# A hybrid attention and DeltaNet layer on one core: gate columns loaded first, the inverse doubled for both chunks at once, scores in two passes

## The chip, the cores and the metric

The kernel runs on one core of a Trainium2 chip. The core has a matrix engine (TensorE, PE in the profile) and three elementwise engines (VectorE or DVE, ScalarE or ACT, GpSimd or POOL). SyncE (SP) issues DMAs. Each engine takes its instructions in the order in which they were written. Times are device microseconds (us) of one execution; the runs of the kernel before took 190.68, 192.27 and 193.10 us, median 192.27.

## What is computed

One decoder layer on x of 256 tokens by 1,024 columns. x is normalised and multiplied with one matrix `w_in` of 4,104 columns, which holds ten inputs: q, k, v, z of eight attention heads (`aq`, `ak`, `av`, `az`, 512 columns each), q, k, v, z of four DeltaNet heads (`dq`, `dk`, `dv`, `dz`, 512 each), and eight gate columns.

```python
h = rms_norm(x, norm_pre_w)
proj = h @ w_in
moba_out = moba_attention(q, k, v) * silu(a_z)        # causal softmax with ALiBi, 8 heads of 64
qkv = silu(causal_depthwise_conv(concat([d_q, d_k, d_v]), conv_w))
beta = sigmoid(d_b)
g = -exp(a_log) * softplus(d_a + dt_bias)
o = gated_delta_rule(q, k, v, g, beta)                # 4 heads of 128, chunked
gdn_out = rms_norm(o, gdn_norm_w) * silu(d_z)
mixed = concat([moba_out, gdn_out]) @ w_out
return x + rms_norm(mixed, norm_post_w)
```

In the delta rule each chunk needs the inverse of a unit lower triangular matrix, and the decays between its tokens:

```python
decay = exp(where(causal, gc[:, None] - gc[None, :], -inf))    # gc: cumulated g
a = where(strict, (k * beta) @ k.T * decay, 0)
t_inv = triangular_solve(a + eye, eye)
```

## The kernel before

The kernel uses two chunks of 128 tokens (t = 0, 1) and writes all work into a plan (`Plan.record`, line 149). `Plan.order` simulates the engines with its own costs, latencies and clock model, ranks what is ready, and `Plan.emit` writes every instruction in the order found. So the order of the code below is not the order of the engines' queues; each is an outcome of the planner, and nearly all instructions have the line of the helper, L364, in the profile. They are told apart by the names of their tiles.

Precision is kept by splitting fp32 operands into two fp32r parts, `hi` (an ACT copy) and `lo` (a DVE subtraction), and by three matmuls per product: hi by hi, hi by lo, lo by hi. A product of plain fp32 operands is one instruction in the code and two records in the profile.

Head (lines 421 to 568). SP loads x in four halves, `wrow` (the norm weight, as one row), then the last 264 columns of `w_in` in four pieces (`dz_raw`): 256 columns of z and the eight gate columns. 18 matmuls of zeros (`ps_warm`) are marked `late`, to be used when PE has nothing else. GpSimd builds all constants: identity, triangles, the masks `blk`, `blks`, `lvl`, the attention bias `bias0`, `qscale`, and later `sel`. The norm weight is spread over the partitions by two matmuls (`ps_w`), DVE scales x by it and by the row's rsqrt (lines 555 to 557), PE transposes the sixteen 128x128 blocks of x (`hT`), and ACT and DVE evict them as `hhi` and `hlo`, 512 columns at a time.

Projections. `dz_piece(1)` (line 628) multiplies the 264 gate and z columns; `dz_piece(0)`, called at line 898, loads and multiplies the other 256 z columns. `proj_group` (line 590) does 512 columns in 96 matmuls; its weights come as two loads of 1 MB, `raw`, from four buffers.

Gates and decay (lines 654 to 702). A chain of small instructions gives `bet` and `gneg`. For each chunk the exponents `ps_d` come from one bf16 matmul for the upper triangle and, per head, a DVE product `gs` of `strl` with the head's gate and an fp32 matmul of `gs` with `triu`.

Inverse (lines 768 to 872). `msk` (GpSimd) and `cmp` pick the 16x16 diagonal blocks, `ps_gb` spreads their rows, and DVE inverts all blocks of both chunks in 15 steps of a product (`wprod`) and a sum (`wc`). `wT` holds the inverse, `xX` its transpose. Then blocks are doubled from 16 to 32, 64 and 128: for each chunk by itself, PE makes `ps_y`, ACT copies it to `yz`, PE makes `ps_w` and DVE subtracts it from `wT`. `xX` is kept up in the same way with products `ps_x` of its own. GpSimd makes the masked `ns` for the first level and clears `yz`.

Recurrence and attention. Lines 901 to 953 run the two chunks of the delta rule (`ps_p`, `ps_S`, `ps_o`). For attention (lines 956 to 1022) `ps_s` holds a head's scores: for the first 128 queries one fp32 matmul, for the other 128 three fp32r matmuls (`qh` by `kh`, `qh` by `kl`, `ql` by `kh`). Both use 64 of the 128 array rows, as a head has 64 channels. Softmax is DVE and ACT work; `ps_pt` are transposes of the weights.

End. `w_out` comes in four loads of 1 MB; `ps_out` adds up the DeltaNet half first, then the attention half. The norm, the residual x and the stores follow, all stores from SP's queue.

Of the kernel before, what the change touches and what calls it, by code (L numbers as in the profile page):

```python
# [8 lines left out]
F32 = mybir.dt.float32  # L9
# [102 lines left out]
class Op:  # L112
    __slots__ = ("n", "eng", "call", "args", "kw", "cost", "table", "preds", "succs", "bufs", "start", "end", "pin", "late", "boost", "work", "load", "pass_")
# [10 lines left out]
class Plan:  # L124
# [9 lines left out]
    def __init__(self):  # L134
        self.ops, self.slots, self.counts, self.boost = [], {}, {}, 0
# [13 lines left out]
    def record(self, eng, real, name, args, kw):  # L149
# [6 lines left out]
        op.boost = self.boost  # L156
# [8 lines left out]
        op.work = op.load = op.pass_ = 0.0  # L165
        if eng == "pe":
# [5 lines left out]
            k = views[1].box[0][1] - views[1].box[0][0]  # L172
            op.work = k / P
        op.preds, op.succs, op.bufs = {}, [], []
        if after:
            op.preds[self.ops[-1]] = True
# [19 lines left out]
    def cost(eng, name, views, kw):  # L196
# [11 lines left out]
        if eng == "dve":  # L208
            if name == "tensor_reduce":
                n = max(v.size() for v in views)  # L210
            ap = 60 * (name == "tensor_scalar" and len(views) > 2 or name == "scalar_tensor_tensor" and n > 64)
# [10 lines left out]
        row = (v.box[-1][1] - v.box[-1][0]) * 4  # L222
        return max(400, (v.box[0][1] - v.box[0][0]) * v.size() * 4 / (370 if row >= 2048 else 220))

    def run(self, rank, banks, reverse=False):
# [26 lines left out]
        table, load, last = None, 1.0, 0.0  # L252
        window, done, cold, share, self.low = 0, {}, True, 1.0, 1.0
        for _ in range(len(ops)):
            best = None
            for e, todo in ready.items():
                cand = []
                for op in todo:
                    t = max(at[op], free[e])
                    if e == "pe":  # L260
                        t = max(t, last + op.load)
# [8 lines left out]
                if not cand:  # L270
# [3 lines left out]
                    (c for c in cand if c[0] <= t0 + (SLACK if e == "pe" else 1)),  # L274
                    key=lambda c: (-1e9 if c[1].pin else 1e9 if c[1].late else rank[c[1]] - c[1].boost 
# [13 lines left out]
            c = op.cost  # L289
            if op.eng == "pe" and not reverse:  # L290
# [79 lines left out]
SLACK = 20  # L370
TABLE = 2000
# [4 lines left out]
GATES = 1  # L376
WARM = 18
# [3 lines left out]
def tile_hybrid(  # L381
# [32 lines left out]
    w_cols = w_in[0].rearrange("(kt p) n -> p kt n", p=P)  # L414
# [3 lines left out]
    wrow = sl("s4", [1, D], "wrow")  # L418
    sv = const([49, P], "sv")
# [3 lines left out]
    dz_raw = plan.tile(sb, [P, KT, PIECE + 2 * HG], F32, "raw_dz1", tag="raw", bufs=RAW_BUFS)  # L423
    HD = D // 2
    for t in range(NT):
# [10 lines left out]

    KH = KT // 2
    GROUP = 2 * PIECE
# [11 lines left out]
    wz = const([P, 256], "wz", BF16)  # L450
    V.memset(wz, 0.0, pin=True)
    pz = bank([P, 512], "ps_warm")
    for i in range(WARM):
        PE.matmul(pz[:, :256], wz[:, :P], wz[:, :256], start=True, stop=True, late=True)


    ident = const([P, P], "ident")
# [10 lines left out]
    blk = const([P, NB, BASE], "blk")  # L468
    G.memset(blk, 1.0)
    G.affine_select(out=blk, in_=blk, pattern=[[-BASE, NB], [0, BASE]], compare_op=OP.is_ge,  # L470
                    fill=0.0, base=0, channel_multiplier=1)
    G.affine_select(out=blk, in_=blk, pattern=[[BASE, NB], [0, BASE]], compare_op=OP.is_ge,
                    fill=0.0, base=BASE - 1, channel_multiplier=-1)

    blks = const([P, NB, BASE], "blks")
    G.affine_select(out=blks, in_=blk, pattern=[[BASE, NB], [1, BASE]], compare_op=OP.is_gt,
                    fill=0.0, base=0, channel_multiplier=-1)

# [649 lines left out]
```

## Time and profile before

| what | value |
|---|---|
| median of three runs | 192.27 us |
| profiled execution | 193.22 us |
| its span, first to last instruction | 191.5 us |
| mean granted PE clock | 0.917 |
| matmul records | 1,337 |
| moved by DMA | 24.92 MB, mean 130 GB/s |

The span leaves out about 1.7 us around the program. Busy times of PE are pipelined spans, so the pace of a run of matmuls is better read from the chain of work: its length over its number of records. The granted clock is the share of full speed that PE was given; at 0.5 a matmul takes twice as long. A row of stretches gives busy time by engine, with the number of instructions in brackets.

### The profile page before, as it was taken

The page shows a single profiled execution, that of the slowest core. Times are in us where ns is not written, and L with a number is a line of the kernel's source. Part 1 is how long each engine was busy: PE and PEld are TensorE (multiplying, and loading weights), DVE is VectorE, ACT ScalarE, POOL GpSimd, SP SyncE. Part 2 cuts the span into 40 slices and gives each one's busy share as a digit, 9 for nine tenths or more (in the row PEclk, how much of TensorE's full clock was granted, in tenths as well). Part 3 has the DMA queues.
Part 4 walks back from the last instruction along what each step waited for, and adds up shares of the span by engine and source line. Part 5 has one row for each costly group of instructions (what it writes and reads, how often), then busy time and mean ns, then how long its engine had stood idle before and what let it go on. Part 6 is the DMA issues. An engine that isn't in the chain of part 4 may idle for free.

```text
span 191.5 us, 3512 instructions
## 1 busy us (share of the span) xinstructions
PE 179.7 (94%) x1337; PEld 163.5 (85%) x1337; DVE 132.5 (69%) x327; ACT 102.1 (53%) x215; POOL 26.4 (14%) x60
## 2 busy tenths in 40 slices
PE   6879999999979999999999999999999999999970
PEld 3359999999969999878977999999888999888860
DVE  3679479995999999984122377627849997725463
ACT  4446499679555666332110364426768989632230
POOL 8546000000580030000000031500000000000100
PEclk9955999999999999997555699999999999999999
DMA  5878998479821634492710000651290000630023
GB/s 168 240 258 242 270 341 295 109 172 259 241 62 23 196 73 151 87 246 109 163 56 3 0 0 3 219 173 46 104 338 0 5 0 0 203 129 0 0 110 110
DMA packets 13448, 24.92 MB, mean 130 GB/s; under 512 B 582, under 2 KB 2935, under 8 KB 13432
## 3 DMA queue, kind: packets, MB, share of 16 engines
q1 hardware_dynamic: 13432, 24.71, 43.5%
q8 instruction: 10, 0.16, 0.3%
q14 instruction: 6, 0.05, 0.1%
HBM read 23.65 MB, written 1.05 MB: 129 GB/s over the span
## 4 chain that ended last, share of the span: by engine, by line
PE 69%; DVE 14%; issue 5%; DMA 4%; ACT 3%; SPq 3%; POOLq 0%; POOL 0%; DVEq 0%
PE ps_out L364 9%; PE ps_ak L364 6%; PE ps_az L364 6%; PE ps_dk L364 6%; PE ps_aq L364 6%; PE ps_av L364 6%; PE ps_dz L364 4%; DMA sv<-in_gdn_norm_w_dram 4%; PE ps_w L364 4%; PE ps_dq L364 3%; PE ps_y L364 3%; PE ps_s L364 3%; SPq L364 3%; DVE y_dv L364 2%; PE ps_gb L364 2%
## 5 line engine op out<-in xcount | busy, mean ns | idle before, releaser
L364 DVE TENSOR_TENSOR o_lo<-raw_o,o_hi 128x1024 fp32r<-128x1024 f32 x8 | 9.8, 1224 | 5.6 <-ACT o_hi L364 5.6
L364 ACT ACTIVATE o_hi<-raw_o 128x1024 fp32r<-128x1024 f32 x8 | 8.5, 1058 | 5.1 <-PE ps_out L364 4.8
L364 ACT ACTIVATE yz<-ps_y 32x128 f32<-32x128 f32 (+2 forms) x8 | 2.6, 324 | 16.0 <-PE ps_w L364 8.9
L364 ACT ACT_TABLE_LOAD x8 | 10.3, 1283 | 0.9 <-PEq L1115 0.8
L364 DVE TENSOR_TENSOR wT<-wT,ps_w 32x128 f32<-32x128 f32 (+2 forms) x8 | 2.8, 349 | 11.1 <-PE ps_w L364 10.0
L364 PE MATMUL ps_dz<-dz_lo,hhi 128*128 128x264 f32 (+1 forms) x32 | 10.4, 326 | 0.0
L364 PE MATMUL ps_dz<-dz_hi,hhi 128*128 128x264 f32 (+1 forms) x32 | 10.3, 321 | 0.0
L364 PE MATMUL ps_dz<-dz_hi,hlo 128*128 128x264 f32 (+1 forms) x32 | 10.0, 312 | 0.0
L364 PEld LDWEIGHTS ps_w<-wT,yz 32*32 32x32 f32 (+2 forms) x64 | 7.9, 207 | 2.4 <-issue 1.3
L364 POOL TENSOR_TENSOR pr<-pr,pow-1_89 128x1 f32<-128x1 f32 x2 | 1.1, 558 | 63.3 <-DVE pr L364 63.3
L364 PE MATMUL ps_az<-hlo,az_hi 128*128 128x256 f32 x32 | 9.5, 297 | 0.0
L364 PE MATMUL ps_az<-hhi,az_hi 128*128 128x256 f32 x32 | 9.5, 295 | 0.0
L364 PE MATMUL ps_az<-hhi,az_lo 128*128 128x256 f32 x32 | 9.3, 290 | 0.0
L364 PE MATMUL ps_ak<-hhi,ak_lo 128*128 128x256 f32 x32 | 9.2, 287 | 0.0
L364 PE MATMUL ps_dv<-hlo,dv_hi 128*128 128x256 f32 x32 | 9.2, 286 | 0.0
L364 PE MATMUL ps_dq<-hhi,dq_hi 128*128 128x256 f32 x32 | 9.2, 286 | 0.0
L364 PE MATMUL ps_aq<-hhi,aq_hi 128*128 128x256 f32 x32 | 9.1, 286 | 0.0
L364 PE MATMUL ps_dq<-hhi,dq_lo 128*128 128x256 f32 x32 | 9.1, 284 | 0.0
L364 PE MATMUL ps_ak<-hhi,ak_hi 128*128 128x256 f32 x32 | 9.1, 284 | 0.0
L364 PE MATMUL ps_ak<-hlo,ak_hi 128*128 128x256 f32 x32 | 9.1, 283 | 0.0
L364 PE MATMUL ps_aq<-hlo,aq_hi 128*128 128x256 f32 x32 | 9.0, 282 | 0.0
L364 PE MATMUL ps_aq<-hhi,aq_lo 128*128 128x256 f32 x32 | 9.0, 282 | 0.0
(264 smaller groups left out, 669.4 us busy)
## 6 DMA issues: line engine op xcount, KB each, us to landing
raw_o<-in_w_out_dram SPq DMA_DIRECT2D x4, 1024.0 KB, 5.0
raw_dk<-in_w_in_dram SPq DMA_DIRECT2D x2, 1024.0 KB, 10.2
raw_dq<-in_w_in_dram SPq DMA_DIRECT2D x2, 1024.0 KB, 11.0
raw_dv<-in_w_in_dram SPq DMA_DIRECT2D x2, 1024.0 KB, 10.2
raw_av<-in_w_in_dram SPq DMA_DIRECT2D x2, 1024.0 KB, 8.3
raw_aq<-in_w_in_dram SPq DMA_DIRECT2D x2, 1024.0 KB, 5.9
raw_ak<-in_w_in_dram SPq DMA_DIRECT2D x2, 1024.0 KB, 6.6
raw_az<-in_w_in_dram SPq DMA_DIRECT2D x2, 1024.0 KB
```

What stands on the lines that cost most here:

```text
L364: op.call(*args, **kw)
```

## The change

1. *Head.* All 520 columns of `dz` and gates come first, in eight loads with rows of 2,080 bytes. `w_in`'s rows are dealt to partitions as `(p kt)` instead of `(kt p)`, so x is transposed with a step of eight columns and the norm weight is a value per partition (`wcol`), applied in the eviction of each 128x128 block. The matmuls `ps_w` and the scaling of x by them go; x is scaled by the row's rsqrt alone, half on ACT and half on DVE. 48 late matmuls instead of 18.
2. *GpSimd's constants.* The masks, the bias, `qscale` and the clearing of `yz` wait for a small copy (`held`) of the gate columns. `sel` is now an ACT copy of the identity.
3. *Decay.* The gates are split into two fp32r parts; per chunk and part one DVE product of 512 columns and one fp32r matmul.
4. *Masks.* `msk` and `ns` are made by DVE instead of GpSimd.
5. *Doubling.* Both chunks in each instruction (eight heads). The `ps_x` products go; `xX` is made by DVE transposes of `wT`.
6. *Scores.* A head's q hi and q lo stand on the two halves of the partitions, k hi on both, k lo on one with zeros on the other: each query block takes two fp32r matmuls over 128 rows.
7. *End.* The second store of each chunk is issued from ACT's queue.
8. *Planner.* Margins on every hand-over, a price for a change of the array rows used, other DMA costs, and leads by stage (`LEAD`) in place of one boost for the gates.

```diff
+LEAD = {"out0": 3258, "dk": 12754, "inv": -3594, "dbl": -402, "out1": -1204, "att0": -192, "mixd": 1425, "az": -11589, "dz": -5411, "gates": 158, "vt": -3052}
-WARM = 18
+SWITCH = 90
+BATCH = 752
+MARGIN = [411, 175, 0]
+WARM = 48
...
-    w_cols = w_in[0].rearrange("(kt p) n -> p kt n", p=P)
+    w_cols = w_in[0].rearrange("(p kt) n -> p kt n", p=P)
...
-    for t in range(NT):
-        for c0 in (0, HD):
-            SP.dma_start(xs[t][:, c0 : c0 + HD], x[0, t * P : (t + 1) * P, c0 : c0 + HD], pin=True)
-        if t == 0:
-            SP.dma_start(wrow, norm_pre_w, pin=True)
-    for k in range(0, KT, 2):
-        SP.dma_start(dz_raw[:, k : k + 2, :], w_cols[:, k : k + 2, 3840:], pin=True)
+    for t in range(NT):
+        SP.dma_start(xs[t], x[0, t * P : (t + 1) * P, :], pin=True)
+    SP.dma_start(wcol, norm_pre_w[0].rearrange("(p kt) -> p kt", kt=KT), pin=True)
+    for k in range(KT):
+        SP.dma_start(dz_raw[k // KH][:, k % KH, :], w_cols[:, k, 3584:], pin=True)
...
-        for i in range(2):
-            xh = xs[t][:, i * HD : (i + 1) * HD]
-            V.scalar_tensor_tensor(xh, xh, r, wps[i], op0=OP.mult, op1=OP.mult)
+        A.activation(xs[t][:, :HD], xs[t][:, :HD], AF.Copy, scale=r)
+        V.tensor_scalar(xs[t][:, HD:], xs[t][:, HD:], r, None, op0=OP.mult)
...
-            A.activation(hhi[at], ps, AF.Copy)
-            V.tensor_tensor(hlo[at], ps, hhi[at], OP.subtract)
+                w = wcol[:, kt : kt + 1]
+                A.activation(hhi[at], ps[:, k, :], AF.Copy, scale=w)
+                V.scalar_tensor_tensor(hlo[at], ps[:, k, :], w, hhi[at], op0=OP.mult, op1=OP.subtract)
...
+            for t in range(NT):
+                token_mms(z1[t], zh[:, k, PIECE:], zl[:, k, PIECE:], kt, t, st, sp)
+            for t in range(NT):
+                token_mms(z0[:, t, :], zh[:, k, :PIECE], zl[:, k, :PIECE], kt, t, st and t == 0, sp and t == NT - 1)
...
+    G.tensor_copy(const([P, 2 * HG], "held"), ba[:, 0, :])
+    now = plan.ops[-1]
...
-        PE.matmul(pd, ident16, far16[:, None, :].to_broadcast(HB), start=True, stop=False)
-        for h in range(HG):
-            V.tensor_scalar(gs[:, h, :], strl, gneg[:, t, h : h + 1], None, op0=OP.mult)
-            PE.matmul(pd[:, h, :], gs[:, h, :], triu, start=False, stop=h == HG - 1)
+        for i in range(2):
+            gs = gsa[i][:, of_chunk[t], :]
+            V.tensor_tensor(gs, triu[:, None, :].to_broadcast(HB), gpart[i][:, t, :, None].to_broadcast(HB), OP.mult)
+            PE.matmul(pd, strl, gs, start=i == 0, stop=False)
+        PE.matmul(pd, ident16, far16[:, None, :].to_broadcast(HB), start=False, stop=True)
...
+    py = bank([P, NH, 64], "ps_y16")
+    for h in range(NH):
+        PE.matmul(py[:, h, :], nsa[:, h, :], head_cols(xXa, 0, h), start=True, stop=True)
+    A.activation(half_cols(yz16, 0), py.rearrange("p h (n s) -> p h n s", n=n), AF.Copy)
+    pw = bank([P, NH, 64], "ps_w16")
+    for h in range(NH):
+        PE.matmul(pw[:, h, :], yz16[:, h, :], head_cols(wTa, 1, h), start=True, stop=True)
+    hc = half_cols(wTa, 1)
+    V.tensor_tensor(hc, hc, pw.rearrange("p h (n s) -> p h n s", n=n), OP.subtract)
+    for t in range(NT):
+        transpose32(t)
...
+        V.tensor_tensor(wTa[r1, :, r2], wTa[r1, :, r2], pw[r1], OP.subtract)
+        if b == 0:
+            V.transpose(xXa[r2, :, r1], wTa[r1, :, r2])
...
+            for e in range(2):
+                b, b2 = own[e], own[1 - e]
+                ps, qs_ = qps[half][b, c, :], qscale[b, m : m + 1]
+                A.activation(q[b, e, :], ps, AF.Copy, scale=qs_)
+                V.scalar_tensor_tensor(q[b2, e, :], ps, qs_, q[b, e, :], op0=OP.mult, op1=OP.subtract)
+                ps = kps[half][b, c, :]
+                A.activation(kh[b, e, :], ps, AF.Copy)
+                A.activation(kh[b2, e, :], ps, AF.Copy)
+                V.tensor_tensor(kl[b, e, :], ps, kh[b, e, :], OP.subtract)
...
-                PE.matmul(ps_s[:, :P], qa[b, m, :], ka[b, m, :], start=True, stop=True)
-                PE.matmul(ps_s[:, P:], qh[b, m, :], kh[b, m, :], start=True, stop=False)
-                PE.matmul(ps_s[:, P:], qh[b, m, :], kl[b, m, :], start=False, stop=False)
-                PE.matmul(ps_s[:, P:], ql[b, m, :], kh[b, m, :], start=False, stop=True)
+                for o, ts, ks in ((ps_s[:, :P], slice(0, P), slice(0, P)), (ps_s[:, P:], slice(P, T), slice(0, T))):
+                    PE.matmul(o, q[:, ts], kh[:, ks], start=True, stop=False)
+                    PE.matmul(o, q[:, ts], kl[:, ks], start=False, stop=True)
...
-            SP.dma_start(out[0, t * P : (t + 1) * P, cs], u[:, cs])
+            (AQ if i == 1 else SP).dma_start(out[0, t * P : (t + 1) * P, cs], u[:, cs])
```

More of the change, by code (lines that the diff above doesn't have):

```diff
@@ L112 @@
 class Op:
-    __slots__ = ("n", "eng", "call", "args", "kw", "cost", "table", "preds", "succs", "bufs", "start", "end", "pin", "late", "boost", "work", "load", "pass_")
+    __slots__ = ("n", "eng", "call", "args", "kw", "cost", "table", "preds", "succs", "bufs", "start", "end", "pin", "late", "boost", "work", "load", "pass_", "stage", "rows")
 class Queue:
@@ L466, in tile_hybrid @@
                     fill=0.0, base=0, channel_multiplier=-1)
[L468 to L477, printed above, removed]
-    strl = const([P, P], "strl")
+    strl = const([P, P], "strl", F32R)
     G.affine_select(out=strl, in_=ones, pattern=[[-1, P]], compare_op=OP.is_gt,
@@ L539, in tile_hybrid @@
     cols = columns(sv, 49, "cols")
-    wps = [bank([P, HD], f"ps_w{i}") for i in range(2)]
-    for i in range(2):
-        PE.matmul(wps[i], ones[0:1, :], wrow[:, i * HD : (i + 1) * HD], start=True, stop=True)
     ssq = const([P, NT, 2], "ssq")
@@ L605, in proj_group, with token_mms, token_piece @@
         return pss
-    def token_piece(raw, n, name, fine):
+    def token_mms(o, hi, lo, kt, t, first, last):
+        ts = slice(t * P, (t + 1) * P)
+        PE.matmul(o, hhi[:, kt, ts], hi, start=first, stop=False)
+        PE.matmul(o, hhi[:, kt, ts], lo, start=False, stop=False)
+        PE.matmul(o, hlo[:, kt, ts], hi, start=False, stop=last)
+    def token_piece(raw, n, name, kn, fine):
         banks = [bank([P, n], f"ps_{name}_{t}") for t in range(NT)]
-        kn = 2 if n > 2 * PIECE - 1 else KH
         for kg in range(0, KT, kn):
@@ new lines, in tile_hybrid @@
+    nl = P // (2 * BASE)
+    lvl = const([P, nl, 2, BASE], "lvl")
+    G.memset(lvl[:, :, 0, :], 0.0, after=now)
+    G.memset(lvl[:, :, 1, :], 1.0, after=now)
+    G.affine_select(out=lvl[:, :, 1, :], in_=lvl[:, :, 1, :], pattern=[[-2 * BASE, nl], [0, BASE]],
+                    compare_op=OP.is_ge, fill=0.0, base=0, channel_multiplier=1, after=now)
+    G.affine_select(out=lvl[:, :, 1, :], in_=lvl[:, :, 1, :], pattern=[[2 * BASE, nl], [0, BASE]],
+                    compare_op=OP.is_ge, fill=0.0, base=BASE - 1, channel_multiplier=-1, after=now)
@@ L643, in tile_hybrid @@
+    slopes = [2.0 ** -(h + 1) for h in range(HA)]
+    qscale = const([P, HA // 2], "qscale")
+    for h in range(HA):
+        b = DA * (h % 2)
+        G.memset(qscale[b : b + DA, h // 2 : h // 2 + 1], (DA ** -0.5) / slopes[h], after=now)
+    for t in range(NT):
+        G.memset(yz16[:, of_chunk[t], :], 0.0, after=now)
     vh = const([P, NT, HA * DA], "vh", F32R)
@@ L875, in tile_hybrid @@
+    H = P // 2
+    yz = sl("yz", [P, NH, H], "yz64")
+    py = bank([P, NH, H], "ps_y64")
+    for h in range(NH):
+        PE.matmul(py[H:, h, :], bTa[:H, h, H:], xXa[:H, h, :H], start=True, stop=True)
+    A.activation(yz[H:], py[H:], AF.Copy)
+    pw = bank([P, NH, H], "ps_w64")
+    for h in range(NH):
+        PE.matmul(pw[:H, h, :], yz[H:, h, :], wTa[H:, h, H:], start=True, stop=True)
+    V.tensor_tensor(wTa[:H, :, H:], wTa[:H, :, H:], pw[:H], OP.subtract)
+    plan.stage = "dq"
     conv_proj(0, qT, "dq")
+    plan.stage = "qn"
```

316 lines of the change are left out of this document (149 added, 167 removed).

## The prediction

> **What bounds the kernel now.** I read the page's line of engines first, then the busy time by stretches (once cut at every change of the granted clock, once in tens), then the chain of work that ended last, then rows of single instructions where an edit needs a price.
>
> ```profile
> PE 179.7 (94%) x1337; PEld 163.5 (85%) x1337; DVE 132.5 (69%) x327; ACT 102.1 (53%) x215; POOL 26.4 (14%) x60
> ...
> 0.00:6.19 6.19, 4.74 (x19) 2.55 (x20) 2.37 (x9) 2.67 (x5) 5.42 (x28) 1.00 0.61 184
> 6.19:9.60 3.41, 2.53 (x8) 0.97 (x8) 2.31 (x6) 1.38 (x4) 1.46 (x8) 1.00 0.89 240
> 9.60:19.84 10.24, 9.14 (x39) 7.99 (x40) 9.21 (x15) 5.37 (x9) 4.91 (x4) 0.50 0.82 251
> 19.84:88.11 68.27, 66.39 (x537) 63.89 (x536) 58.97 (x152) 43.45 (x83) 8.69 (x7) 1.00 0.65 182
> 88.11:108.59 20.48, 20.04 (x163) 16.84 (x162) 5.76 (x14) 3.20 (x8) 0.00 (x0) 0.50 0.21 53
> 108.59:185.50 76.91, 76.89 (x578) 71.29 (x577) 51.76 (x129) 45.54 (x108) 5.41 (x13) 1.00 0.24 83
> ```
>
> The columns are the stretch, its length, the busy time of PE, weight loads, DVE, ACT and POOL (instructions in brackets), the granted clock, and the DMA's share and GB/s. PE is busy in 66.39 of 68.27, 20.04 of 20.48 and 76.89 of 76.91 us: the time is PE's work over its clock, with a start and a tail around it. Two stretches, 10.24 and 20.48 us, stand at half clock: together they cost at most (10.24 + 20.48) / 2 = 15.4 us. In the second DVE has 5.76 and ACT 3.20 us of work: it is the doubling of the triangular inverse.
>
> ```profile
> 50.00:60.00 10.00, 8.58 (x75) 8.41 (x74) 10.00 (x23) 5.34 (x8) 6.80 (x5) 1.00 0.36 102
> ...
> 70.00:80.00 10.00, 10.00 (x70) 9.12 (x68) 10.00 (x26) 5.69 (x10) 0.00 (x0) 1.00 0.49 120
> ```
>
> Ahead of the doubling DVE is as full as PE, so work taken from PE there pays only if DVE's work can be put off as well. The chain prices PE's parts (start, length, records):
>
> ```profile
> 16.02 7.12 PE ps_dz L364 x44
> 23.14 11.31 PE ps_dk L364 x96
> ...
> 37.75 1.78 PE ps_d L364 x16
> ...
> 84.04 1.97 PE ps_y L364 x16
> 86.01 0.94 PE ps_x L364 x14
> ...
> 91.35 2.32 PE ps_w L364 x10
> 93.68 0.56 PE ps_y L364 x8
> ...
> 95.88 0.29 DVE wT L364
> 96.30 0.60 PE ps_w L364 x8
> ...
> 98.38 1.04 PE ps_y L364 x8
> ...
> 104.66 1.04 PE ps_w L364 x8
> 105.70 2.00 PE ps_p L364 x8
> ...
> 135.94 0.77 PE ps_s L364 x5
> ```
>
> ```profile
> L364 PE MATMUL ps_dz<-dz_hi,hhi x32: 277/283/568, 11.9 to 74.8; 128*128 128x264 f32 x16, 128*128 128x256 f32 x16
> ```
>
> ```profile
> 84.04:105.70 21.66, 5.19 (x9) 2.20 (x9) 0.00 (x0) 0.00 (x0) 0.59 0.35 93
> ```
>
> ```profile
> PE ps_gb L364 <- DVE cmp L364: 1.4, 1, 1.4
> ```
>
> A projection matmul of 256 columns costs 11.31 / 96 = 0.118 us at full clock; an fp32 matmul leaves two records. The first lone row gives the first and last start of a dz matmul, the second what av does while the doubling runs, the third PE's longest wait.
>
> **The change part by part.** The sum is made against the profiled execution: 193.2 us, of which 191.5 are its span and 1.7 lie around it; the median of the runs shown is 192.27, 0.9 below it.
>
> *Head and gates.* Before, the start carried only the 264 gate columns (48 matmuls), and the other 256 columns of the same group ran as 48 matmuls near 75 us as PE's filler. Now all 520 columns come first, in eight loads of 2,080-byte rows. At the rates of the rows above, 240 and 251 GB/s (1.14 MB moved by 6.19 us, 1.96 by 9.60), x (1.05 MB) and the block (2.13 MB) are there at 9.6 + (3.18 - 1.96) / 0.251 = 14.5 us and dk's 2.10 MB at 22.8. Before, the first dz matmul began at 11.9, with the half clock cutting its stream until 19.84. From 11.9 at full clock 96 matmuls take 96 x 0.119 = 11.4 us and end at 23.3, where dk began at 23.14. So the 48 later matmuls (48 x 0.118 = 5.7 us) go, for 0.2 us here. The full clock is to come from 48 filler matmuls instead of 18, which lie where PE waits for x. Loads of dk and everything behind it on SP's queue come about 4.2 us later (1.06 MB / 0.251), dk's first half at 18.7, ahead of its use at 23. Bounds: -5.7 if all goes so, -0.6 if the clock stays at half as in the row 9.60:19.84 (5.1 us lost). I take -5.5.
>
> The norm weight moves into the eviction: DVE loses four scalings of x and four subtractions of 512 and gains two short scalings and 16 instructions of 128; ACT gains 12 evictions and the two sel tiles.
>
> ```profile
> L364 DVE SCALAR_TENSOR_TENSOR x<-x,rx,ps_w 128x512 f32<-128x512 f32 x4 | 3.0, 745 | 0.1
> L364 DVE TENSOR_TENSOR hlo<-hT,hhi 128x512 fp32r<-128x512 f32 x4 | 2.6, 682 | 1.0 <-ACT hhi L364 1.0
> L364 DVE TENSOR_SCALAR gs<-strl,gneg 128x128 f32<-128x128 f32 x8 | 1.6, 277 | 0.0
> L364 DVE TENSOR_TENSOR dT<-ps_kq,dT 128x512 f32<-128x512 f32 x2 | 1.4, 687 | 0.0
> L364 POOL TENSOR_TENSOR msk<-bT,blks 128x512 f32<-128x512 f32 x2 | 2.6, 1290 | 0.2 <-DVE bT L364 0.2
> L364 ACT ACTIVATE qa_h<-ps_aq,qscale 128x128 fp32r<-128x128 f32 x4 | 1.4, 367 | 0.3 <-DVE qa L364 0.3
> L364 ACT ACTIVATE avT<-ps_av 64x256 f32<-64x256 f32 x8 | 3.0, 374 | 0.6 <-PE ps_av L364 0.6
> ```
>
> DVE: -3.0 - 2.6 + 16 x 0.28 + about 0.8 = -0.3 us. ACT: about +5 us (12 near 0.25, two copies near 1), against 4.9 us idle in the row 9.60:19.84. The 16 transposes read x with a step of eight elements, which no row shows: nothing, or twice the 0.11 us of a record of 128 columns (the ps_d row), +1.8; a gain is excluded, as each still reads 128 columns. I take +0.5 for both, near the low end, because PE waits in that stretch anyway (9.14 of 10.24).
>
> *GpSimd.* About 5 of POOL's first 6.9 us (5.42 + 1.46), memsets and selects, move behind a copy that waits for the gate columns (near 24 us). Queued behind it on POOL are only these and the masks' users from 50 us on, so no result is late. The rsqrt of the norm now has an addition ahead of it on POOL. What the move can do is slow DVE:
>
> ```profile
> 10.81 0.70 DVE L364 TENSOR_TENSOR dz_lo<-raw_dz,dz_hi 128x528 fp32r<-128x528 f32 x1
> ...
> 15.87 1.53 POOL L364 TENSOR_SCALAR_AFFINE_SELECT sel<-sel 128x1024 f32<-128x1024 f32 x1
> ...
> 16.55 1.37 DVE L364 TENSOR_TENSOR dz_lo<-raw_dz,dz_hi 128x528 fp32r<-128x528 f32 x1
> ...
> 54.41 0.23 DVE L364 SCALAR_TENSOR_TENSOR cmp<-cmp,emod 128x64 f32<-128x64 f32 x1
> ...
> 56.07 1.27 POOL L364 TENSOR_TENSOR ns<-bT,lvl 128x512 f32<-128x512 f32 x1 [0.28 <-DVE cmp L364]
> ...
> 56.28 1.14 DVE L364 SCALAR_TENSOR_TENSOR cmp<-cmp,emod 128x64 f32<-128x64 f32 x1
> ```
>
> The same DVE instruction took 0.70 and 1.37 us, 0.23 and 1.14 us, the longer time beside a GpSimd instruction. Between 24 and 34 us that could cost DVE 0 to 5 us; the selects of sel (2 x 1.53) and the masks on POOL go, and 0.67 + 0.91 us of stalls with them. I take 0 net.
> [...]
>
> *Decay.* Sixteen records, 1.78 us, become four matmuls of 512 columns, 4 x 0.235 = 0.94: -0.8 on PE. DVE: 8 x 0.20 (one after the other) become 4 x 0.69 and a subtraction: +1.3.
>
> *Masks.* Four multiplications go from POOL (1.29 us each) to DVE: +2.75. The stretch of DVE before the doubling so gets +1.3 + 2.75 - 0.9, less the 2.4 us of the second dz half's two splits (1.21 each), which the head now carries: +0.8, all taken, as DVE is full there.
>
> *Doubling.* Before: 84.04 to 105.70, 21.7 us, with nine av matmuls in it, 5.2 us, so 16.5. After, the 48 ps_x records are gone and eight heads go through each step: at half clock y and w of 16 cost 2 x 1.97 and 16 x 0.232, of 32 four times 0.56 and 0.60, of 64 twice 1.04 and 1.04: 16.4 us; at full clock 8.2. Both chunks now wait together at six hand-overs (about 0.6 us each, as around the wT row at 95.88, 0.29 long with a wait on each side) and two transposes on DVE (near 0.65 each, as long as the 687 ns row), some 5.5 us, which av and aq matmuls can fill. Bounds: -8.3 at full clock with all filled, and with av (2.6) and p (0.8) at full clock too, -11.7; +5.4 at half clock with nothing filled. I take half the time at half clock, hand-overs mostly filled: -5.5, nearer the gain since the row 70.00:80.00 shows PE with filler at hand.
>
> *Scores.* Per head five records, 0.77 us, become two f32r passes of 128 and two of 256 columns over all rows: 2 x 0.06 + 2 x 0.118 = 0.36. Eight heads: -3.3, at least -1.5 where rows of the chain are shorter; I take -2.5. ACT gains per half 12 evictions of 64x256 at 0.37 for four (two as qa_h, two of k, an estimated 1.4 us), +6 in all; DVE eight of 256 near 0.42 for four of 0.28 and one of 0.69, +3.1 in all. Both lie beside 76.9 us in which ACT has 45.5 and DVE 51.8 us of work, with az and the first half of out as PE's cover; without that cover they cost 6. I take +0.7.
>
> *Tail.* The second store of each chunk goes from SP's to ACT's queue. For chunk 0 it waits on ACT for DVE's u, and a square of chunk 1 queued behind it waits too, some 0.2 us, off the end. I take -0.3, an estimate between 0 and the 0.6 of an issue.
>
> *The planner and the loads.* Projection weights keep their 2 KB rows, only dealt to other partitions: 0. New leads, margins and a price for changing rows reorder every queue. PE's idle time in the stretches above adds up to 5.8 us, so a better order alone gains less than that; a worse one has no bound. I take 0, as the longest wait is 1.4.
>
> Sum: -5.5 + 0.5 - 0.8 + 0.8 - 5.5 - 2.5 + 0.7 - 0.3 = -12.6; 193.2 - 12.6 = 180.6 us.
>
> **Rivals.**
> 1. *The clock holds through the doubling.* dk leads, so its inverse starts earlier and more projections are left as filler: the doubling gives -11.7 instead of -5.5, 174.4. For it: DVE is idle for 14.7 of 20.48 us in the doubling. Against: 32-row matmuls fill few of the array's rows.
> 2. *DVE is the bound before the doubling, and both chunks wait together.* PE runs out of filler, the doubling's gain is lost and a wait as before ps_gb comes on top: 180.6 + 5.5 + 1.4 = 187.5. For it: DVE's 10.00 of 10.00 us twice.
> 3. *The clock falls in the head all the same*, after the fillers, when the transposes run. As in 9.60:19.84, 10.24 us at half: the head gives -0.6 instead of -5.5, 185.5. For it: the clock fell 3.4 us after the 18 fillers ended. [...]
> 4. *No gain.* Head and doubling both give nothing (+5.5 and +5.5): 191.6.
> 5. *Slower: the written order calls for the doubling too early.* PE takes its queue in order; if y stands where the planner believes the inverse done while DVE is late, PE stands idle and then runs at half clock. With 12 us of idle time and 10.24 us at half (5.1): 197.7. It decides from about 15.5 us lost, and PE's longest wait now is 1.4.
>
> **How the numbers follow.** Forecast 0.45, rival 1 0.18, rival 2 0.15, rival 3 0.10, rival 4 0.06, rival 5 0.06. The time is the forecast's, 180.6; its own range, 176.5 to 184.5, lets the doubling's share at half clock go from a quarter to three quarters (8.2 x 0.25 = 2 each way) and the other terms 2 more. The range for 8 in 10 leaves out rivals 4 and 5 and the far side of rival 1: 173.0 to 188.5. About 2% is what a measurement of this kernel can tell from no change. Faster by more than that is below 188.4: forecast, rivals 1 and 3 and most of rival 2, 0.83; within 2% 0.11; slower 0.06.
>
> **What would show it.** Head: dz (96 matmuls) ends and dk begins by 24 us at clock 1.0; past 27 the head failed. Decay: four ps_d matmuls. Doubling: no ps_x; from the first y to p under 17 us, and a stretch at half clock of 10.24 us or less. Scores: four ps_s records per head within 0.4 us. PE idle under 5 us from 24 us to the last ps_out, which ends near 173; ACT or DVE as the releaser of PE in the attention would show the added evictions on the path. The prediction is wrong if PE waits for wT for more than 5 us, or if the half clock lasts 20 us again.

## The result, and the profile after

The changed kernel takes 175.55 us (median of four runs, 174.1 to 179.37), the kernel before, run beside it, 192.69 us (190.68 to 193.67). The ratio is 0.912, with a 95% interval of 0.897 to 0.926. The forecast was 180.6 us, in a range of 173.0 to 188.5. Ratios and intervals leave out runs more than 1.5% above the fastest of the same kernel, and medians have every run. Two of the four runs have a mean granted clock of 0.997 (174.1, the profiled one, and 174.55 us); the other two have 0.969 and 0.957 (176.55 and 179.37), so the clock did not hold in every execution.

Two lines of the changed kernel's page, the engines and the granted clock in 40 slices:

```profile
PE 162.5 (94%) x1295; PEld 151.9 (88%) x1295; DVE 138.0 (80%) x337; ACT 112.5 (65%) x246; POOL 22.1 (13%) x61
...
PEclk9999999999999999999999999999999999999998
```

PE is busy for the same 94%, but of 172.3 us instead of 191.5, and no slice before the last shows a fallen clock. The busy time by stretches has the same columns as before. The cuts lie at the first dz matmul, the first dk, near the first av, at the doubling's first y, at the first p behind it, and at the last ps_out; two stretches of 3.41 us inside the doubling follow:

```profile
8.89:23.50 14.61, 14.04 (x114) 13.41 (x113) 9.99 (x29) 11.66 (x29) 1.53 (x7) 1.00 0.71 237
23.50:63.30 39.80, 39.66 (x334) 38.85 (x333) 37.99 (x89) 29.12 (x53) 9.09 (x22) 1.00 0.79 234
63.30:99.30 36.00, 35.90 (x259) 33.42 (x257) 32.73 (x70) 24.28 (x47) 1.90 (x2) 1.00 0.45 150
99.30:118.60 19.30, 18.63 (x210) 17.14 (x211) 18.75 (x54) 14.89 (x39) 0.61 (x2) 1.00 0.35 110
118.60:166.30 47.70, 47.54 (x341) 43.72 (x339) 32.21 (x81) 26.97 (x70) 5.41 (x13) 1.00 0.11 40
106.51:109.93 3.42, 3.01 (x46) 2.34 (x44) 3.38 (x12) 3.26 (x8) 0.35 (x2) 1.00 0.98 325
109.93:113.34 3.41, 3.18 (x45) 2.59 (x45) 3.32 (x11) 3.28 (x10) 0.00 (x0) 1.00 0.13 47
```

The doubling takes 19.3 us, hardly less than the 21.7 before. But 210 matmuls run in it, at clock 1.00, and ACT has 14.89 us of work there, where the 20.48 us at half clock had 3.20: ak, the scores, transposes of the weights, az and av now stand between its steps. DVE has 18.75 of 19.30 us. The waits of PE and the chain (start, length, engine, tile) show who sets the pace there:

```profile
PE hT L373 <- ACT x L373: 1.0, 1, 1.0
PE hT L373 <- ACT hhi L373: 0.6, 1, 0.6
PE ps_y L373 <- DVE xX L373: 0.3, 1, 0.3
PE ps_w L373 <- DVE wT L373: 0.2, 1, 0.2
```

```profile
24.59 11.02 PE ps_dk L373 x94
...
92.66 1.13 DVE az_lo L373
94.62 1.22 DVE az_lo L373
97.27 1.30 DVE wT L373 x2
98.57 1.22 DVE xX L373 x2
...
107.25 0.67 DVE xX L373
```

From 89.5 to 121 us the chain goes through DVE, with PE beside it nearly full: the two engines bound this part together.

To see where 19.2 us of span went, I add up PE's matmuls from start to start. "Work" is that time multiplied by the granted clock, "fillers" the same for ps_warm, "lost" what the half clock added, "idle" the gaps; 1.1 us ahead of the first matmul and 5.9 to 6.1 behind the last come on top in every run. Work includes short waits that the modelled ends hide. The record of the clock begins with its first change, 4.0 to 7.0 us into the span (14.1 in e3), and what lies before it counts as 1.00. Yet in all fourteen profiles the fillers before that change start 213 ns apart, and in the changed kernel those behind it 109 ns: this first part runs at half pace too, and what it loses stands under work and fillers.

```
us                        span   work  fillers  lost  idle   median of runs
before                   191.5  161.4    3.8    14.5   4.6   192.69
after                    172.3  156.0    6.6     0.0   2.6   175.55
e1  no leads             178.6  153.6    8.0     8.5   1.3   180.11
e2  18 fillers           179.1  154.2    4.0     8.1   5.7   180.57
e3  before, 48 fillers   189.0  165.0    7.3     6.8   2.9   191.10
e4  chunks apart         190.6  158.3    7.4    13.7   4.1   193.91
e5  before, new planner  199.2  166.5    3.4    16.9   5.3   198.90
e6  after, filled        181.0  157.4    7.0     5.2   4.3   181.36
e7  before, filled       191.1  167.8    3.1     7.9   5.2   192.79
e8  constants free       171.6  155.2    7.5     0.0   1.7   173.41
e9  old planner          176.9  155.5    7.5     1.7   5.0   179.45
e10 e8, z columns late   173.2  156.7    8.2     0.0   1.1   175.00
e11 e4, old planner      188.5  156.0    7.6    11.8   5.9   190.48
e12 e8, masks on GpSimd  182.3  156.0    7.7     8.5   2.9   183.77
```

Of the 19.2 us, 14.5 are the clock, 5.4 work and 2.0 idle time; 2.8 more fillers are set against them. Pieces of the work that went are the ps_x records (2.6 us of it before), the ps_w matmuls of the norm weight (2.1), the scores (0.9) and the decay (0.65). An edit of the code makes the planner order everything anew, so runs are read by these columns and not by the median alone.

### The profile page after: what moved, and what is told of

The parts are those of the page before. It is cut to its first block, busy times and chain, and to the rows that moved or that the text cites. A ratio compares the mean times of both kernels' runs of the same rounds, so it can differ in the third digit from the quotient of the medians.

```text
span 172.3 us, 3462 instructions
## 1 busy us (share of the span) xinstructions
PE 162.5 (94%) x1295; PEld 151.9 (88%) x1295; DVE 138.0 (80%) x337; ACT 112.5 (65%) x246; POOL 22.1 (13%) x61
## 4 chain that ended last, share of the span: by engine, by line
PE 64%; DVE 18%; ACT 6%; issue 5%; DMA 3%; SPq 1%; POOLq 0%; POOL 0%; DVEq 0%; ACTq 0%
PE ps_out L373 10%; PE ps_av L373 8%; PE ps_dk L373 7%; PE ps_dq L373 6%; PE ps_az L373 6%; PE ps_dz L373 6%; PE ps_dv L373 6%; PE ps_aq L373 5%; DMA raw_dz<-in_w_in_dram 3%; DVE az_lo L373 3%; DVE att_y L373 3%; DVE wT L373 2%; PE ps_gb L373 2%; DVE qz L373 2%; ACT hhi L373 2%
## 5 line engine op out<-in xcount | busy, mean ns | idle before, releaser
L373 ACT ACTIVATE att_y<-att_y,mx 128x128 f32<-128x128 f32 (+1 forms) x16 | 7.1, 445 | 3.3 <-DVE mx L373 3.2
L373 PE MATMUL ps_dv<-hhi,dv_lo 128*128 128x256 f32 x32 | 9.1, 291 | 0.0
L373 PE MATMUL ps_dk<-hhi,dk_hi 128*128 128x256 f32 x32 | 9.1, 286 | 0.0
L373 PE MATMUL ps_dv<-hhi,dv_hi 128*128 128x256 f32 x32 | 9.1, 285 | 0.0
L373 PE MATMUL ps_dz<-dz_lo,hhi 128*128 128x264 f32 (+1 forms) x32 | 9.1, 296 | 0.0
L373 PE MATMUL ps_dq<-hlo,dq_hi 128*128 128x256 f32 x32 | 9.0, 283 | 0.0
L373 PE MATMUL ps_dk<-hlo,dk_hi 128*128 128x256 f32 x32 | 8.9, 279 | 0.0
L373 PE MATMUL ps_warm<-wz 128*128 128x256 bf16 x48 | 7.7, 316 | 1.1 <-DVE wz L373 1.1
```

Of the source, the lines that this page charges most:

```text
L373: op.call(*args, **kw)
```

## The experiments

### Order or batching: what keeps the clock up in the doubling

**e1**, the changed kernel without leads:

```diff
-LEAD = {"out0": 3258, "dk": 12754, "inv": -3594, ...}
+LEAD = {}
```

> The changed kernel with every lead set to nothing; margins, the price for changing rows and all edits stay. Theory A (the clock holds through the doubling because the order puts ak, az, av and attention matmuls between its steps): the inverse moves ahead of them again, a stretch of 10 to 20 us at half clock comes back around ps_y and ps_w, and the time is 175.6 + 5 to 175.6 + 10, that is 180.6 to 185.6 us. Theory B (the clock holds because both chunks are doubled together and ps_x is gone, whatever stands between): no stretch at half clock after 30 us, and the time stays at 174 to 178 us.

Measured: 180.11 us, ratio to before 0.931 (0.924 to 0.938). The stretches of that run, the window ahead of the fall and the fall:

```profile
105.66:109.07 3.41, 2.68 (x29) 2.08 (x28) 3.35 (x11) 1.74 (x6) 0.00 (x0) 1.00 0.00 0
109.07:126.14 17.07, 17.03 (x126) 15.93 (x127) 11.30 (x37) 8.12 (x23) 0.00 (x0) 0.50 0.19 63
```

A stretch of 17.07 us at half clock is back, 8.5 us lost. Theory B falls: batching does not hold the clock under every order. Theory A has the stretch, and nearly the time, but not for its reason: the inverse does not move ahead. Its first y stands at 98.0 us (99.3 in the changed kernel), behind 64 of the 96 ak matmuls (69 there). Why the window ahead of the fall is thin in this order stays open.

**e4**, the changed kernel with the old doubling (for each level, first chunk 0, then chunk 1, with ps_x):

```diff
-    py = bank([P, NH, 64], "ps_y16")
-    for h in range(NH):
-        PE.matmul(py[:, h, :], nsa[:, h, :], head_cols(xXa, 0, h), ...)
+    for t in range(NT):
+        py = bank([P, HG, 64], f"ps_y16_{t}")
+        for h in range(HG):
+            PE.matmul(py[:, h, :], ns[:, h, :], head_cols(xX[t], 0, h), ...)
...
+        px = bank([P, HG, 2 * BASE], f"ps_x16_{t}")
```

> The changed kernel with the doubling done chunk by chunk as before, ps_x products included; planner, leads and all else as changed. Theory A (order): the steps still lie among full-clock matmuls, the clock holds, and only the 48 ps_x records (3.9 us at half clock before, so 2.0 at full) and the smaller hand-overs change: 176 to 179 us. Theory B (batching): the half clock returns for 10 to 20 us: 175.6 + 2 + 5 to 175.6 + 2 + 10, that is 182.6 to 187.6 us.

Measured: 193.91 us, ratio to before 0.999 (0.994 to 1.005). Undoing this one part gives back the whole gain, more than either theory allowed:

```profile
114.45:117.86 3.41, 2.73 (x38) 2.14 (x36) 2.90 (x9) 1.60 (x8) 0.00 (x0) 1.00 0.00 0
117.86:145.17 27.31, 27.24 (x179) 22.73 (x179) 10.41 (x38) 6.90 (x23) 1.90 (x2) 0.50 0.00 1
```

27.3 us at half clock, 13.7 lost. The new leads call the inverse late (its first y at 109.6 us, before at 84.0), and by then all of ak is done: no ak or az matmul stands between its steps. DVE and ACT have 10.41 and 6.90 of 27.31 us.

**e5**, the kernel before with the new planner alone (margins, SWITCH, BATCH, its costs of loads and reductions, LEAD):

> The kernel before with only the planner changed (margins, price for changing rows, DMA costs, the leads by stage); loads, doubling, scores, decay and masks as before, 18 warm matmuls. Theory A (order): the stretch of 20.5 us at half clock in the doubling shrinks to 10 or to nothing and the time falls by 5 to 10 us, to 183 to 188 us. Theory B (batching): the stretch stays and the time is within 3 us of 192.7.

Measured: 198.90 us, ratio 1.019 (1.011 to 1.027). Neither theory: the order alone makes the old body slower. In the profiled run, 201.23 us, the doubling is called at 120 us and stands at half clock for longer than before, 23.89 us instead of 20.48:

```profile
127.74:131.16 3.42, 3.26 (x36) 2.37 (x34) 2.32 (x11) 1.90 (x7) 0.00 (x0) 1.00 0.00 0
131.16:155.05 23.89, 23.89 (x151) 19.24 (x151) 8.86 (x33) 6.62 (x21) 0.00 (x0) 0.50 0.01 2
```

That is not the whole reason: two runs of 196.46 and 196.57 us have a mean clock of 0.943, above the 0.917 of the profile before, and are slower all the same. The table's work is 5.1 us more than before.

**e9**, all edits of the body under the old planner (its costs of loads too):

```diff
-SWITCH = 90
-BATCH = 752
-MARGIN = [411, 175, 0]
...
-LEAD = {"out0": 3258, "dk": 12754, ...}
+SWITCH = 0
+BATCH = 0
+MARGIN = [0, 0, 0]
...
+LEAD = {"gates": 1}
```

> All edits of the changed kernel's body, ordered by the planner of the kernel before (no margins, no price for changing rows, its DMA costs, one lead of 1 for the gates). Theory A (order and batching are both needed): the doubling comes ahead of ak and attention again, a stretch of 10 to 20 us at half clock stands in it, and the time is 180 to 186 us, at or above the 180.1 of the run without leads. Theory B (batching alone does it): within 2 us of 175.6. Theory D (without margins DVE's full queue makes PE wait at the hand-overs as well): over 186 us, with PE idle for more than 6 us.

Measured: 179.45 us, ratio 0.930 (0.924 to 0.936). Its doubling lies where it lay before, with 51 aq matmuls between its steps, and the clock holds there:

```profile
13.11:16.52 3.41, 0.54 (x5) 0.34 (x3) 2.75 (x8) 2.76 (x9) 0.00 (x0) 1.00 0.80 252
16.52:19.93 3.41, 3.41 (x16) 3.13 (x16) 2.69 (x9) 1.48 (x6) 0.00 (x0) 0.50 0.64 241
86.70:102.40 15.70, 15.19 (x187) 14.31 (x188) 10.34 (x16) 4.22 (x7) 2.73 (x2) 1.00 0.38 127
```

```profile
PE ps_cols L373 <- DMA sv<-in_conv_w_dram: 2.9, 1, 2.9
```

So B is right about this doubling and wrong about the time. What the new planner adds is elsewhere: here PE stands 2.9 us behind ps_cols, which waits for a small load, and the clock falls for one window. Idle 5.0 and lost 1.7 against 2.6 and 0.0 after are 4.1 us, the 3.9 between the medians.

**e11**, e4 under the old planner, closes the square.

> All edits of the body except the doubling, which goes chunk by chunk with ps_x as before, under the planner of the kernel before. It closes the square: together and old planner gave 179.45, together and new planner 175.55, apart and new planner 193.9. Theory E (batching itself holds the clock, under either planner): 10 to 20 us at half clock return in the doubling, and with the 2 us of ps_x the time is 186.5 to 191.5. Theory G (apart is bad only where the new planner calls the inverse late, when little dense work is left): the doubling lies where the kernel before had it, ahead of aq and ak, and at most 10 us at half clock return, 181 to 186 us.

Measured: 190.48 us, ratio 0.988 (0.973 to 1.002). Theory E has the time and the stretch:

```profile
88.76:92.17 3.41, 3.13 (x43) 2.75 (x41) 2.34 (x5) 0.38 (x1) 2.46 (x2) 1.00 0.81 255
92.17:112.66 20.49, 20.10 (x166) 18.52 (x167) 5.72 (x15) 3.33 (x11) 0.00 (x0) 0.50 0.09 34
```

Between the steps of this doubling stand 11 aq matmuls, where e9 had 51. With everything else of the body changed, doubling both chunks together is worth 11.0 us under the old planner (190.48 to 179.45) and 18.4 under the new one (193.91 to 175.55). So chunk by chunk the clock fell under both planners. Together it held under both, but not in every order: it fell in e1, and falls in e2, e6 and e12 below.

### Filling the doubling

**e7** puts 20 matmuls of 512 bfloat16 columns into the doubling of the kernel before, **e6** ten into that of the changed kernel:

```diff
+    def fill(k):
+        for _ in range(k):
+            PE.matmul(pf, ident16, far16[:, None, :].to_broadcast([P, HG, P]), start=True, stop=True, after=prev)
...
             PE.matmul(py[:, h, :], ns[:, h, :], half_cols(xX[t], 0, h), start=True, stop=True)
+        fill(2)
```

> The kernel before with 20 extra matmuls of zeros and constants (128x128 by 512 bfloat16 columns) set behind the ps_y, ps_x and ps_w batches of its doubling, two at a time, and nothing else. At full clock they cost at most 20 x 0.21 = 4.3 us of PE. Theory C (the clock falls where too few matmul columns run in a stretch of 3.41 us, whatever the engines wait for): the 20.5 us at half clock in the doubling shrink to 10 or to nothing; with the hand-overs as cover the time falls by 10.2 - 4.3 = 6 us, to about 187 us (183 to 189). Rival: the clock follows the small shapes of the doubling themselves or the waits; then the stretch stays and the time rises by 4 to 9 us, to 197 to 202 us.

Measured: 187.83 to 192.86 us in four runs, median 192.79. In the profiled run the fall that came at 88.1 us comes at 96.7, two and a half windows of 3.41 us later, and the half clock of the doubling shrinks from 20.48 to 10.24 us:

```profile
82.70:96.68 13.98, 13.68 (x166) 10.58 (x167) 4.98 (x15) 1.85 (x6) 1.90 (x2) 1.00 0.26 71
96.68:106.92 10.24, 10.24 (x50) 7.58 (x49) 2.53 (x4) 1.81 (x3) 0.00 (x0) 0.50 0.00 0
```

The one run whose mean clock was 0.997 took 187.83, the time that theory C gives; the profiled one took 192.85, as its work grew by 6.4 us and what it lost fell by 6.6, of which 1.7 lie in the head, which the edit leaves alone (6.83 us at half clock instead of 10.24). The fall comes later with more matmuls, and in the median the empty matmuls cost what they save.

> The changed kernel with ten such extra matmuls behind the batches of its doubling. Theory C: its thinnest stretches (106 to 113 us) are filled up, no run falls to half clock there any more, and the time is 174 to 176 us in every run, where the runs of the changed kernel spread from 174.1 to 179.4. Rival: PE has no time to spare there and the ten cost 10 x 0.21 = 2.1 us and more: 177 to 178 us.

Measured: 181.36 us (180.88 to 182.74), ratio 0.946 (0.940 to 0.953): worse than even the rival. The ten stand on the chain of an inverse that was tight with DVE. In the profiled run the doubling begins 3.7 us later, at 103.0 us, and takes 26.9 us to the first p instead of 19.3; PE waits 0.6 and 0.8 us for DVE inside it, and the clock falls all the same, for 10.24 us.

### The head

**e2** (after with `WARM = 18`) and **e3** (before with `WARM = 48`) change the number of fillers alone:

> The changed kernel with 18 late filler matmuls instead of 48. If the fillers keep the clock in the head, a stretch of about 10 us at half clock returns before 24 us as it stood before (9.6 to 19.8 us), dk begins 3 to 5 us later, and the time is 178.6 to 180.6 us. Rival: the stream of 96 dz matmuls, early and unbroken, keeps the clock by itself; then the time stays within 1 us of 175.6.

Measured: 176.31 to 180.91 us, median 180.57. With the block of 520 columns first but few fillers the clock falls in the head, for 6.83 us, and dk begins at 25.7 instead of 23.5:

```profile
5.46:8.88 3.42, 1.37 (x9) 1.18 (x10) 2.37 (x6) 2.96 (x7) 1.22 (x3) 1.00 0.57 225
8.88:15.71 6.83, 6.03 (x29) 5.69 (x28) 4.24 (x13) 5.04 (x15) 0.00 (x0) 0.50 0.72 235
```

So the early stream does not keep the clock by itself. In the profiled run (180.85 us) it fell in the doubling too, for 10.24 us; the run of 176.31 had a mean clock of 0.972 against 0.944. That run is 1.8 to 2.2 us above the two of the changed kernel at 0.997, about dk's delay: the median reaches the first theory's range only with the fall in the doubling.

> The kernel before with 48 late filler matmuls instead of 18. If the fillers alone keep the clock in the head, the stretch of 10.2 us at half clock (9.6 to 19.8) goes and the time falls by up to 5.1 us, to 187.6. Rival: the loads set the head; PE waits for x and the gate columns whatever its clock, and the time stays within 1.5 us of 192.7. What happens in the doubling decides the rest: a stretch of 20.5 us there as before.

Measured: 185.37 to 191.43 us, median 191.10, between the two theories. The record of the profiled run shows no fall in the head, and dk begins at 20.2 instead of 23.0. Yet the transposes of x there still run at half pace:

```profile
L364 PE MATMUL hT<-ident,x x16: 415/421/475, 9.7 to 13.6; 128*128 128x128 f32 x16
```

In the changed kernel, at full clock, one takes 273 ns at the least and 276 in the median. The record of the clock holds changes only: in this run the core had not come up to full clock before 14.1 us, with four single-row ps_w matmuls ahead. Its "lost" in the table lacks that part, and its "work" contains it: two runs of nearly its time (191.22 and 191.43 us, its own 190.99) have a mean clock of 0.927, where its record gives 0.962.

Nor do the fillers bring dk forward here. The planner puts 17 of them before 16 us, as in the kernel before, and 24 of the new ones between the steps of the doubling, where the half clock is 13.65 us instead of 20.48. And in e7, whose edit leaves the head alone, dk begins at 20.3 us as well: the old head gives 20.2 to 23.0 us, by where the half clock falls in it. So e3 does not answer its question, and is one more filling of the doubling.

**e10**, on the base of e8 (below), brings back the head with 264 gate columns first and 256 z columns later, with 48 fillers:

```diff
-        SP.dma_start(dz_raw[k // KH][:, k % KH, :], w_cols[:, k, 3584:], pin=True)
+        SP.dma_start(dz_raw[:, k : k + 2, :], w_cols[:, k : k + 2, 3840:], pin=True)
...
+    plan.stage = "dz0"
+    dz_piece(0)
```

> The changed kernel with GpSimd's constants free (173.4 us) as base, and with the head of the kernel before: only the 264 gate columns come first, in 1,056-byte rows; the other 256 z columns are loaded and multiplied later in 48 matmuls. If the head's term of the prediction is right in size (5.5 us, from the half clock that stood in its dz stream), the time is 178 to 180 us. Theory W (the 48 fillers keep the clock, so the early block saves nothing but the wait for its columns): dk begins 2 to 4 us earlier, the 48 matmuls come back as 5.7 us of PE work later, and the time is 174.5 to 177 us. Theory F (the late 48 matmuls are useful as PE's cover in the doubling): 173 to 174.5 us.

Measured: 175.00 us, ratio 0.909 (0.904 to 0.913). Theory W has the time: dk begins at 18.5 us, five earlier, the 48 matmuls come back later, and the clock never falls. The block first is worth 1.6 us (175.00 to 173.41).

### GpSimd

**e8** frees the constants (every `after=now` goes):

> The changed kernel with GpSimd's constants no longer held back behind the gate columns, so that they run in the first 10 us beside the loads and DVE's work on x. Theory P (the placing costs and gains nothing, as the prediction took it): within 1.5 us of 175.6. Theory Q (it keeps DVE free in the head): the splits of dz and the scaling of x get longer beside GpSimd, dk begins 1 to 3 us later, 177 to 179 us. [...]

Measured: 173.41 us (173.20 to 173.51), ratio 0.904 (0.899 to 0.909), the fastest kernel of all, below the ranges of theories P and Q. Compared at full clock, spans 171.6 and 172.3, the gain is 0.7 us; the rest of the medians' difference lies in runs of the changed kernel whose mean clock was lower (0.969 and 0.957 in two of four). The selects of the bias, first with the constants held, then free:

```profile
27.83 2.33 POOL L373 TENSOR_SCALAR_AFFINE_SELECT bias<-bias 128x128 f32<-128x128 f32 x2
```

```profile
7.17 0.46 POOL L373 TENSOR_SCALAR_AFFINE_SELECT bias<-bias 128x128 f32<-128x128 f32 x1
...
7.76 0.40 POOL L373 TENSOR_SCALAR_AFFINE_SELECT bias<-bias 128x256 f32<-128x256 f32 x1
```

Held, two of them take 2.33 us beside DVE's splits of dk; free, 0.86, beside DVE's work on x. At this place it is GpSimd's instructions that are longer: DVE's two pairs of splits take 2.39 and 2.45 us with the constants held and 2.36 each without. In the prediction's rows of the kernel before it was DVE's (0.70 and 1.37 us, 0.23 and 1.14), so either engine's can be the longer.

**e12**, on the base of e8, gives msk and ns back to GpSimd (`V.tensor_tensor` to `G.tensor_tensor` in four places):

> The changed kernel with GpSimd's constants free (173.4 us) as base, and the four masked products of msk and ns back on GpSimd. If DVE sets the pace between 40 and 130 us, as its nearly full queue there suggests, the 2.75 us that leave it come off the path in part: 171 to 172.7 us. If PE sets it and DVE is only full beside it: 173 to 174 us. If GpSimd's 1.3 us each stretch DVE's own instructions (0.70 to 1.37, 0.23 to 1.14 us beside GpSimd in the kernel before), or stand on the chain from bT to the inverse: 174 to 176 us.

Measured: 183.77 us (183.71 to 184.04), ratio 0.959 (0.952 to 0.966), 10.4 us slower than its base: far beyond all three theories. DVE's rows in it (start, length):

```profile
61.72 1.22 DVE L373 TENSOR_TENSOR av_lo<-raw_av,av_hi 128x1024 fp32r<-128x1024 f32 x1 [3.48 <-ACT av_hi L373]
62.86 0.34 DVE L373 SCALAR_TENSOR_TENSOR bT<-ps_kk,dd,dT 128x128 f32<-128x128 f32 x1
...
65.85 1.71 DVE L373 TENSOR_TENSOR aq_lo<-raw_aq,aq_hi 128x1024 fp32r<-128x1024 f32 x1
...
71.73 1.16 DVE L373 SCALAR_TENSOR_TENSOR cmp<-cmp,emod 128x64 f32<-128x64 f32 x1
...
73.20 1.96 DVE L373 TENSOR_TENSOR aq_lo<-raw_aq,aq_hi 128x1024 fp32r<-128x1024 f32 x1
```

and, for the first bT, a split and the last cmp, those of the base:

```profile
58.33 0.32 DVE L373 SCALAR_TENSOR_TENSOR bT<-ps_kk,dd,dT 128x128 f32<-128x128 f32 x1
...
66.56 1.22 DVE L373 TENSOR_TENSOR aq_lo<-raw_aq,aq_hi 128x1024 fp32r<-128x1024 f32 x1
67.69 0.22 DVE L373 SCALAR_TENSOR_TENSOR cmp<-cmp,emod 128x64 f32<-128x64 f32 x1
```

The last cmp ends at 72.9 instead of 67.9 us. The masks explain little of that. Each takes 1.30 on GpSimd instead of 0.68 on DVE, and DVE's own instructions grow beside it (1.22 to 1.71 and 1.96, 0.22 to 1.16). But the first bT, which stands ahead of every mask, is already 4.5 us late: in the order of this run DVE stands idle for 3.48 us before it, behind a split that waits for ACT's av_hi. The doubling begins at 101.8 instead of 96.2, with 15 ak matmuls left to stand in it instead of 35, and then the clock falls:

```profile
112.33:115.74 3.41, 2.68 (x34) 2.00 (x34) 3.23 (x11) 2.90 (x8) 0.00 (x0) 1.00 0.38 145
115.74:132.80 17.06, 17.06 (x93) 14.71 (x94) 9.38 (x31) 5.82 (x20) 0.00 (x0) 0.50 0.00 1
```

8.5 us of the 10.4 are the half clock. So this run prices an order and not the masks, which can answer for half a microsecond of the five; what they cost on GpSimd in the order of the base stays open.

### What lets the clock fall

In all fourteen profiles the changes of the granted clock lie whole multiples of 3.41 us apart. Cut at that grid, each window at full clock can be given a number: the columns that its matmuls stream, counted twice for an fp32 record (in the kernel before a 128-column one takes 0.111 us, ps_d's 1.78 us over 16, and a 256-column one of fp32r 0.118, dk's pace), transposes included, and weighted by the rows used out of 128. At that pace a window holds about 7,400.

```
windows at full clock that end before the last matmul    631
with 3,200 or more: then a fall                            0 of 611
with fewer: then a fall                                   17 of 20
ahead of a fall: before 2,880 (doubling), e1 2,816, e4 1,600,
  e5 3,072, e6 2,960, e7 3,184, e11 2,624, e12 2,432
no fall: e9 2,944, e6 3,056, after 3,136 (at 109.9 us)
```

In these counts the limit lies near 43% of dk's pace (3,200 of 7,400), and PE's busy time does not show it: 3.13 of 3.41 us in e11, then a fall, 3.01 and 3.18 after, and none. Without the weight by rows the count fails: 58 windows that held lie at or below the highest that fell, with it three. (Weighted by the array's columns as well it does no worse, so the count does not say which of the two it is.) The thin windows of the doublings hold matmuls of 32 and 64 rows and hand-overs: 2,880 columns by that weight in the window from 84.7 us of the kernel before, 832 to 2,048 in the four at half clock behind it. With 51 aq matmuls between the steps of both chunks together the clock held (e9), with 11 between those of chunk by chunk it fell (e11). The changed kernel passes its two thin windows narrowly, with 3,328 and 3,136. In the profiles of its body with leads the doublings that begin at 96.2, 96.5 and 99.3 us (e8, e10, after) keep the clock, and those at 101.4, 101.8 and 103.0 (e2, e12, e6) lose it. All this is shown by count, not by a run that changes nothing else; why a window of 2,944 holds (e9) and one of 3,184 does not (e7) stays open.

## Why the prediction was right, and where it was not

The direction, the side of 2% and the range were right; the likeliest time was 5.0 us too high. Rival 1, given 0.18, is what the clock did in the profiled execution: 174.4 forecast for it, 174.1 measured. Its reason is not: the inverse does not start earlier but later (first y at 99.3 us, before 84.0), behind all of aq and 69 of 96 ak matmuls, and what fills it is put there by the order. That the two times agree so well is in part luck, since terms that were off make up for each other (norm weight and scores below).

*Doubling, −5.5, half the time at half clock.* This term was mis-sized. In the profiled execution the half clock went altogether (20.48 us before, 0 after), where the term kept half of it. Full-clock PE time of y and w is 8.0 us, as forecast (8.2). The argument against rival 1, that 32-row matmuls fill few rows, fits the runs (3,328 and 3,136 in the two thin windows, 2,816 in e1, 1,600 in e4, 2,432 in e12), but the term took what else runs in the doubling from the old trace, av matmuls, and not from what the new order would put there. The argument for it, that DVE was idle in the doubling, missed the point: DVE is full there now. From the first y to p it takes 19.3 us and not under 17, since the steps are spread among other work, not slowed. (Its hand-overs, six of 0.6 and two transposes of 0.65, add up to 4.9 and not 5.5.)

*Planner, 0, "less than 5.8".* Wrong step: only PE's idle time was weighed, not where the order puts sparse work. Under the changed body the planner is worth 3.9 us (e9); on the old body it costs 1.9% (e5). Its worth depends on the batching, and that of the batching on it (11.0 or 18.4).

*Head, −5.5.* The size fits, the cause was half right. The clock holds and dz ends at 23.3 as said. But e10 puts "the 48 later matmuls go" at 1.6 us. Fillers bring dk's start forward by 2.2 (e2, 25.7 to 23.5). The rest lies between the old head, where dk began at 20.2 to 23.0 as the half clock fell (e3, e7, before), and e10's 18.5 with as few columns; fillers, norm weight and order share it, and no run separates them. Rival 3 is in part what happens with 18 fillers: 6.83 us at half clock, not 10.24. And the clock of 1.00 that the working reads in the row 0.00:6.19 is no record: the fillers there start 213 ns apart, at half pace.

*Norm weight, +0.5.* The strided transposes cost nothing: 276 ns median against 272 at the least before. PE's four ps_w matmuls (2.1 us) were left out of the sum, and the other way the scores gave 1.6 less than forecast.

*GpSimd's constants, 0.* Measured 0.7 us against the change (e8), near the low end of the 0 to 5 us of DVE's time that the prediction estimated. Beside DVE's splits of dk GpSimd's selects were longer (2.33 us for 0.86) and DVE's splits hardly (2.39 and 2.45 for 2.36).

*Masks, +0.8.* DVE's part is as priced (0.68 each, four make 2.7). What it costs or saves in time no run shows: e12, without them on DVE, loses 10.4, but by its order.

*Decay, −0.8.* Four matmuls as said; 1.13 us for 1.78, so −0.65.

*Scores, −2.5 and +0.7.* Four records a head as said, but 4.2 us in all against 5.1, −0.9: the rows are interleaved with other work. No wait of PE for ACT or DVE of attention over 0.2 us is left, so the +0.7 is not seen either.

*Tail, −0.3.* Nothing: 6.0 us behind the last matmul before and after. The 0.6 of an issue was the author's estimate: the stores' issues in the kernel before take 0.33 to 0.40 us, 0.42 to 0.67 from one to the next. Rival 2, DVE as bound, is half there: DVE carries the chain from 89.5 to 121 us, but PE's longest wait for it is 0.3. Rivals 4 and 5 did not occur; e4 ends where 4 does, and e5 is slower as 5 has it, though not by its wait: PE idles 5.3 us in all, not 12.

## What to carry to other kernels

Ask of a half-clock stretch not how to shorten it but which dense matmuls can stand between its steps (51 of aq in e9, where the clock held, 11 in e11, where it fell), and start the chain that leads to it early enough that some are left. A wait off the bottleneck engine can cost several times its length where it decides when such a stretch begins (e12: DVE idle for 3.5 us, 10.4 us lost). Where an edit changes the order of everything, find the first instruction that is late before the edit is blamed. Two parts of a change that meet in one stage are not priced one by one: here the planner is worth −3.9 us with the batching and costs time without it.

## What the runs showed of the hardware

In these runs the falls go with a window's row-weighted columns and not with PE's busy time: every one of the 17 falls ahead of the last matmul came behind a window with fewer than 3,200, while PE was busy for 3.13 of 3.41 us ahead of one fall (e11) and for 3.01 and 3.18 in two windows that held (after). A stretch at half clock lasted from one window (3.41 us, e9) to eight (27.3 us, e4): of the windows at half clock, the 45 with half clock behind them hold 3,200 at most, and 15 of the 17 that end such a stretch 3,328 or more. The counts fit better with the transposes in them: without them, 15 windows that held lie at or below the highest that fell (in e1 the one from 6.7 us, with 2,320 columns beside 16 transposes; in the changed kernel the one from 106.5 us, with 2,304); with them, three do. The record of the clock shows 1.00 until its first change while matmuls run at half pace (fillers 213 ns apart, behind it 109 in the changed kernel), for 4.0 to 7.0 us in thirteen profiles and until 14.1 us in e3, so the pace of a known matmul is to be read beside it.
